# Half of the first 40 up blocks in plain f32, 16 activations kept on chip, and lists, gathers and loads re-paced

## The chip, the cores and the metric

The kernel runs on one core of one Trainium2 chip. The metric is the device time of one execution in microseconds (us); several executions are timed and their median is taken. One more execution is recorded by the hardware profiler, and every row below is from that one.

## The reference

One decoder layer over 512 tokens of width 1024. First comes attention with its output product and a layer norm; the change does not touch that part. Then comes a memory of 16384 experts, of which every token uses 16 for each of 8 heads:

```python
q = (hx @ w_pq).reshape(PEER_CHUNK, PEER_HEADS, 2, PEER_HALF)
sc = jnp.einsum('thpd,hpnd->thpn', q, sub_keys).astype(jnp.float32)
v_half, i_half = lax.top_k(sc, PEER_TOPK)
cand = v_half[:, :, 0, :, None] + v_half[:, :, 1, None, :]
...
top_s, top_pos = lax.top_k(cand, PEER_TOPK)
idx = jnp.take_along_axis(cand_idx, top_pos, axis=-1)
g = jax.nn.softmax(top_s, axis=-1)
a = jax.nn.gelu(jnp.einsum('thkd,td->thk', u_tab[idx], hx), approximate=False)
return jnp.einsum('thk,thkd->td', (g * a).astype(hx.dtype), v_tab[idx])
```

The layer ends with a second layer norm of `alpha * x + gate2 * ffn`.

## The kernel before, in words

The expert part treats the tokens in two ways. For 128 tokens ("tile 0") and for 64 tokens ("the half tile") the chosen rows of `u_tab` and `v_tab` are gathered: GpSimd (POOL) issues one indirect DMA of 128 rows (512 KB) into one of five buffers `gb`, and VectorE (DVE) makes one dot product with it (L746, for u) or one multiply-add into `acc0` (L782, for v). The half tile needs 64 dots only, tile 0 needs 128 dots and 128 multiply-adds. For the other 320 tokens (and for the v side of the half tile, so 384 there) the kernel computes all experts densely, in 128 blocks of 128 experts:

- **U loop.** For each block e the rows `u_T[e]` are loaded to `raw` (SP queue, three buffers). ScalarE (ACT) rounds them to `hi` (fp32r), DVE makes `lo = raw - hi` (three buffers each; an instruction carries the line of the helper, L86 and L87). TensorE (PE) multiplies three times for each of 8 slices of the width (hi by h2h, hi by h2l, lo by h2h; `mm3`, L96 to L98), 24 matmuls of 128x320 into a bank `st`, of which there are four. ACT takes the gelu (L812). The first NB = 32 results stay on chip as `a_r`; the other 96 (`a_s`) are written to DRAM (`a_d`).
- **Beside the U loop** generators are pulled by amounts of a budget for each block: `tk` makes the four lists of chosen experts (token tiles in the order 1, 2, 3, 0, all on DVE), `gt` issues the gathers with their dots (the half tile as soon as list 1 is there, tile 0 when list 0 is there), and `gg` builds the dense weights g of tiles 2, 3 and 1 with one-hot products (DVE `oh`, ACT `go` and `stage`, PE f32 matmuls at L692) and writes them to `g_d`.
- **V loop.** For each block n, in the order of a list `order`, `v_blk` is loaded to `raw` and split as above. The weights of a group of 8 blocks come with one DMA of 1.5 MB from `g_d` on ACT's queue (`gl`, two buffers), issued one group ahead. ACT and DVE make `w = a * gl` (the a comes from `a_r`, or from DRAM by `a_b`), then `wh` and `wl`, and PE does 18 matmuls of 128x512 into six banks that are kept over all blocks.
- **End.** For the last six blocks all splits are made first; the last four go to `hi4` and `lo4`. PE then completes one token tile after the other, and `finish` does the layer norm of each on DVE. `finish(0)`, of tile 0, is given out at n = 116, after all the remaining multiply-adds.

Each engine runs its instructions in one order, set when the program is built, and waits at each for what it reads and for free buffers.

Of the kernel before, what the change touches and what calls it, by code (L numbers as in the profile page):

```python
# [20 lines left out]
P = 128  # L21
# [12 lines left out]
ALPHA = 2.0 ** 0.25  # L34
LAM0 = 0.8 - 0.6 * math.exp(-0.0)
LOWEST = -3.0e38
NB = 32
GB = 8
NS = 96
GRATE = 0.52  # L40
HU = 64
T0U = P + HU
TU = S - T0U
LAST = 6
GBUF = 5
RA = 1.7
RB = 1.9


@with_exitstack  # L50
def layer(ctx: ExitStack, tc: tile.TileContext, A, out, dbg=None):
# [43 lines left out]
    def mm3(ps, lh, ll, rh, rl, first, last):  # L95
        nc.tensor.matmul(ps, lh, rh, start=first, stop=False)  # L96
        nc.tensor.matmul(ps, lh, rl, start=False, stop=False)  # L97
        nc.tensor.matmul(ps, ll, rh, start=False, stop=last)  # L98
# [76 lines left out]
    def drain(g, n=None):  # L175
        i = 0
        while n is None or i < n:
            try:
                next(g)
            except StopIteration:  # L180
                return False
            i += 1
        return True
# [391 lines left out]
    def u_split(e):  # L575
        return split(load_raw(A["u_T"][e], [P, KB, P]), [P, KB, P])

    prev = None
    for b in range(16):
        raw = load_raw(A["w_pqT"][b], [P, KB, P])  # L580
        hi, lo = split(raw, [P, KB, P])
        ps = bank()
        for k in range(KB):
            mm3(ps, hi[:, k, :], lo[:, k, :], h2h[:, k, :], h2l[:, k, :], k == 0, k == KB - 1)
        qT = pq.tile([P, S], F32, name="qT", tag="qT", bufs=3)
        nc.scalar.copy(qT, ps)
        if b >= 14:
            early[b - 14] = u_split(b - 14)
        if prev:
            scores(*prev)  # L590
        prev = (b, qT)
# [208 lines left out]
        return us  # L800

    def u_block(e):
        hi, lo = early.pop(e) if e in early else u_split(e)
        ps = psq[0].tile([P, TU], F32, name="st", tag="st", bufs=psq[1])
        for k in range(KB):
            mm3(ps, hi[:, k, :], lo[:, k, :], h2h[:, k, T0U:], h2l[:, k, T0U:], k == 0, k == KB - 1)
        pace[0], pace_next[0] = pace_next[0], split.last
        if NB <= e < NB + NS:
            a = ring.tile([P, TU], F32, name="a_s", tag="a_s", bufs=3)
        else:  # L810
            a = ring.tile([P, TU], F32, name="a_r", tag="a_r", bufs=NB)
        nc.scalar.activation(a, ps, AF.Gelu)  # L812
        acts[e] = a

    def keep(e):
        if NB <= e < NB + NS:
            nc.scalar.dma_start(a_d[e - NB], acts[e])
            acts[e] = None

    g_stack = ExitStack()  # L820
    gp = g_stack.enter_context(tc.tile_pool(name="gp", bufs=1, reuse_waits="tile"))
    tk = all_topk(gp)
    gg = all_g(gp, tk)
    c1 = c2 = 0.0
    gt = gathers()
    for e in range(NB + NS):
        u_block(e)
        keep(e)
        budget[0] = pull(tk, budget[0] + (2.6 if 1 not in best else 1.6))
        if 2 in best:  # L830
            c1 += GRATE
            while c1 >= 1.0:
                c1 -= 1.0
                drain(gg, 1)
        if 1 in lists:
            c2 = pull(gt, c2 + (RA if not weighted else RB))
    pull(tk, 1e9)
    while not weighted:
        next(gt)
    drain(gg)  # L840
    g_stack.close()
    sel_stack.close()
    psB_stack.close()
    psq[:] = ctx.enter_context(tc.tile_pool(name="psC", bufs=1, space=bass.MemoryType.PSUM, reuse_waits="tile")), 2, 6

# [3 lines left out]
    order = list(range(NB)) + list(range(NB + NS, NKEY)) + list(range(NB, NB + NS))  # L849

    def g_load(e):
        gl = vp.tile([P, NTG, GB * TG], F32, name="gl", tag="gl", bufs=2)
        nc.scalar.dma_start(gl, g_d.rearrange("g p i t -> p g (i t)")[:, :, e * TG:(e + GB) * TG])
        return gl

# [37 lines left out]
    for n in range(NKEY):  # L893
        if n % GB == 0 and n + GB < NKEY:
            gls[order[n + GB]] = g_load(order[n + GB])
        if n + NB + NS < NKEY:
            u_block(n + NB + NS)
            c2 = pull(gt, c2 + 3.6)
        else:
            c2 = pull(gt, c2 + 1.6)  # L900
        if n == NKEY - 16:
            ring_stack.close()
            fin = ctx.enter_context(tc.tile_pool(name="fin", bufs=1, side="right", reuse_waits="tile"))
# [114 lines left out]
```

## Time and profile before

| what | value |
|---|---|
| median of 3 runs | 1553.13 us (1549.42 to 1555.18) |
| the profiled execution, device time | 1551.68 us |
| its span, first to last instruction | 1549.9 us |
| busy in the span | PE 1432.2, DVE 1267.8, ACT 826.1, POOL 466.8 us |
| moved by DMA | 451.43 MB, mean 291 GB/s |

The span falls into stages: up to about 360 us attention, the queries and their scores; from 360 to about 981 us the U loop; from there to about 1540 us the V loop and its end. A busy time is the union of an engine's instructions, so an engine that is busy for a whole stretch may be what sets its length; "idle before" in a row is the time that the engine stood still just ahead of the instruction, with what ended it.

### The profile page before, as it was taken

How to read it: one execution, taken by the hardware profiler on the slowest of the kernel's cores; microseconds unless marked ns; L12 is line 12 of the kernel's file. 1: busy time of each engine (PE TensorE's matmuls, PEld its weight loads, DVE VectorE, ACT ScalarE, POOL GpSimd, SP SyncE). 2: the span in 40 equal slices, each digit the busy share in tenths (PEclk: the TensorE clock that was granted, in tenths of full speed). 3: DMA queues.
4: the chain of work that ended last, by engine and by line, in shares of the span. 5: the costliest groups of instructions: out<-in, count | busy, mean ns of one | idle time of the engine just before them, and what ended most of it. 6: DMA issues, size and time to landing. Idle time of an engine off the chain costs nothing.

```text
span 1549.9 us, 22874 instructions
## 1 busy us (share of the span) xinstructions
PE 1432.2 (92%) x7837; PEld 1254.3 (81%) x7837; DVE 1267.8 (82%) x2606; ACT 826.1 (53%) x1523; POOL 466.8 (30%) x338
## 2 busy tenths in 40 slices
PE   6999998998688899999999969999989999989996
PEld 5777776888687889999999969888868778868884
DVE  7897676999888998798879848989778788879766
ACT  2465534334357889899799834344333343334440
POOL 0000000000433334454544525545434443532000
PEclk9999998999999999999999989999989999999998
DMA  8856363222767789999999999999999999999751
GB/s 312 289 182 200 130 212 103 83 85 92 250 239 283 238 310 375 357 408 394 416 342 390 405 362 409 382 379 346 340 385 342 368 372 355 363 337 362 233 171 48
DMA packets 184855, 451.43 MB, mean 291 GB/s; under 512 B 15841, under 2 KB 90977, under 8 KB 181538
## 3 DMA queue, kind: packets, MB, share of 16 engines
q1 hardware_dynamic: 75426, 241.28, 43.0%
q0 software_dynamic: 46080, 167.79, 28.9%
q10 hardware_dynamic: 63232, 40.90, 8.7%
q8 instruction: 61, 1.00, 0.3%
q14 instruction: 56, 0.46, 0.1%
HBM read 404.00 MB, written 45.88 MB: 290 GB/s over the span
## 4 chain that ended last, share of the span: by engine, by line
PE 47%; issue 14%; DMA 13%; DVE 11%; POOL 8%; ACT 5%; POOLq 0%; SPq 0%; DVEq 0%; ACTq 0%
POOL gb L741 8%; PE acc L97 7%; PE acc L98 7%; PE acc L96 7%; DMA raw<-v_blk 5%; PE bank L96 5%; PE bank L97 4%; PE bank L98 4%; DMA gl<-g_d 3%; DMA raw<-u_T 3%; DVE lo L87 3%; PE st L96 2%; PE st L98 2%; PE st L97 2%; ACT hi L86 2%
## 5 line engine op out<-in xcount | busy, mean ns | idle before, releaser
L86 ACT CAST hi<-raw 128x1024 fp32r<-128x1024 f32 x286 | 299.8, 1050 | 333.5 <-DMA raw<-v_blk 111.4
L87 DVE TENSOR_TENSOR lo<-raw,hi 128x1024 fp32r<-128x1024 f32 x286 | 348.7, 1221 | 119.0 <-ACT hi L86 113.4
L96 PE MATMUL st<-h2h,hi 128*128 128x320 f32 x1024 | 326.3, 319 | 27.6 <-ACT hi L86 27.6
L98 PE MATMUL st<-h2h,lo 128*128 128x320 f32 x1024 | 322.0, 316 | 17.5 <-DVE lo L87 17.5
L97 PE MATMUL st<-h2l,hi 128*128 128x320 f32 x1024 | 321.7, 314 | 0.0
L96 PE MATMUL acc<-hi,wh 128*128 128x512 f32 x768 | 302.2, 394 | 17.3 <-ACT hi L86 17.0
L97 PE MATMUL acc<-lo,wh 128*128 128x512 f32 x768 | 303.8, 396 | 5.0 <-DVE lo L87 4.6
L98 PE MATMUL acc<-hi,wl 128*128 128x512 f32 x768 | 301.8, 393 | 0.0
L741 POOL DMA_INDIRECT gb<-v_tab,ei x128 | 182.4, 1425 | 240.2 <-DVE acc L782 222.3
L746 DVE SCALAR_TENSOR_TENSOR gb<-gb,h2n 128x1024 f32<-128x1024 f32 x192 | 230.7, 1218 | 21.2 <-DMA gb<-u_tab,ei 15.4
L741 POOL DMA_INDIRECT gb<-u_tab,ei x128 | 183.4, 1433 | 196.5 <-DVE gb L746 182.1
L96 PEld LDWEIGHTS st<-h2h,hi 128*128 128x128 f32 x1024 | 196.5, 192 | 31.2 <-ACT hi L86 31.2
L98 PEld LDWEIGHTS st<-h2h,lo 128*128 128x128 f32 x1024 | 196.0, 192 | 20.5 <-DVE lo L87 20.5
L97 PEld LDWEIGHTS st<-h2l,hi 128*128 128x128 f32 x1024 | 196.3, 192 | 0.0
L96 PEld LDWEIGHTS acc<-hi,wh 128*128 128x128 f32 x768 | 145.9, 190 | 49.8 <-ACT hi L86 18.7
L97 PEld LDWEIGHTS acc<-lo,wh 128*128 128x128 f32 x768 | 145.8, 190 | 41.7 <-DVE lo L87 10.4
L688 ACT ACTIVATE go<-oh,iT 128x128 f32<-128x128 bf16 x384 | 169.7, 525 | 9.4 <-DVE oh L682 7.5
L741 POOL DMA_INDIRECT gb<-u_tab,eip x64 | 91.0, 1422 | 272.1 <-ACT hi L86 148.7
L98 PEld LDWEIGHTS acc<-hi,wl 128*128 128x128 f32 x768 | 145.9, 190 | 30.3
L782 DVE SCALAR_TENSOR_TENSOR acc<-gb,w,acc 128x1024 f32<-128x1024 f32 x127 | 162.2, 1277 | 0.0
L104 POOL TENSOR_TENSOR rs_r<-rs_v,mhalf 128x1 f32<-128x1 f32 (+1 forms) x12 | 9.3, 775 | 364.1 <-DVE rs_v L102 328.3
L692 PE MATMUL acc<-go,oh 128*128 128x128 f32 x768 | 108.5, 284 | 7.3 <-ACT go L688 7.1
(213 smaller groups left out, 1988.9 us busy)
## 6 DMA issues: line engine op xcount, KB each, us to landing
raw<-u_T SPq DMA_DIRECT2D x128, 512.0 KB
raw<-v_blk SPq DMA_DIRECT2D x128, 512.0 KB
wada<-w_adaT SPq DMA_DIRECT2D x48, 512.0 KB
g_d<-stage SPq DMA_DIRECT2D x24, 1024.0 KB
gl<-g_d ACTq DMA_DIRECT2D x16, 1536.0 KB
a_d<-a_s ACTq DMA_DIRECT2D x96, 160.0 KB
a_b<-a_d SPq DMA_DIRECT2D x96, 160.0 KB
raw<-w_pqT SPq DMA_DIRECT2D x16, 512.0 KB
```

The lines of the kernel that those rows point to most:

```text
L86: nc.scalar.copy(hi, src)
L87: split.last = nc.vector.tensor_sub(lo, src, hi.bitcast(F32))
L96: nc.tensor.matmul(ps, lh, rh, start=first, stop=False)
L97: nc.tensor.matmul(ps, lh, rl, start=False, stop=False)
L98: nc.tensor.matmul(ps, ll, rh, start=False, stop=last)
L104: nc.gpsimd.tensor_tensor(r, v, mhalf.to_broadcast([P, n]), op=OP.pow)
L688: nc.scalar.activation(go[:, i, :], oh0[:, :, i], AF.Copy, scale=iT[:, 2, t0 + i:t0 + i + 1])
L692: nc.tensor.matmul(ps[:, i * P:(i + 1) * P], oh1[:, 4 * u + i, :], go[:, 4 * u + i, :], start=True, stop=True)
L741: nc.gpsimd.indirect_dma_start(out=b, out_offset=None, in_=A[tab], in_offset=bass.IndirectOffsetOnAxis(ap=idx[:, j:j + 1], axis=0))
L746: paced(nc.vector.scalar_tensor_tensor(b, b, 1.0, h2n, op0=OP.mult, op1=OP.mult, accum_out=acc))
L782: paced(nc.vector.scalar_tensor_tensor(acc0, b, w0[:, j:j + 1], acc0, op0=OP.mult, op1=OP.add))
```

## The change

- Of the first 40 U blocks (`PLAIN`) the odd ones are not split. PE multiplies the loaded `raw`, as f32, by `h2f`, an f32 copy of the activations: 8 f32 matmuls of 128x320 where there were 24 fp32r ones, no `hi` on ACT, no `lo` on DVE. `h2f` is made once by a DVE addition over 128x2560. The two blocks that are split early, in the stage of the queries, are now 0 and 2.
- NB goes from 32 to 24 and NS from 96 to 88. The last 16 U blocks keep their results on chip (`a_l`, in memory that the lists and g leave free at e = 112), so 88 results go through DRAM. In the V loop the order is 24 from `a_r`, 16 from `a_l`, 88 from DRAM.
- After list 2 is made the lists are pulled at 0.7 a block (before 1.6), so lists 3 and 0 come later. The build of g goes at 0.54 (before 0.52), the half tile's dots at 1.6 (1.7), tile 0's multiply-adds in the V loop at 1.45 (1.6).
- `gl` has one buffer for groups with an even number; odd groups are loaded to `gl2`, in the memory that h2h had. The numbers of the groups in their order are 0, 1, 2, 14, 15, 3, 4, and so on, so that groups 2 and 14 share one buffer, one after the other, and so do 15 and 3. `hi4` has that same memory.

```diff
@@ -34,17 +34,19 @@
 ALPHA = 2.0 ** 0.25
 LAM0 = 0.8 - 0.6 * math.exp(-0.0)
 LOWEST = -3.0e38
-NB = 32
+NB = 24
 GB = 8
-NS = 96
-GRATE = 0.52
+NS = 88
+GRATE = 0.54
 HU = 64
 T0U = P + HU
 TU = S - T0U
 LAST = 6
 GBUF = 5
-RA = 1.7
+RA = 1.6
 RB = 1.9
+RV = 1.45
+PLAIN = 40
 
 
 @with_exitstack
@@ -585,7 +587,7 @@
         qT = pq.tile([P, S], F32, name="qT", tag="qT", bufs=3)
         nc.scalar.copy(qT, ps)
         if b >= 14:
-            early[b - 14] = u_split(b - 14)
+            early[2 * b - 28] = u_split(2 * b - 28)
         if prev:
             scores(*prev)
         prev = (b, qT)
@@ -800,15 +802,22 @@
         return us
 
     def u_block(e):
-        hi, lo = early.pop(e) if e in early else u_split(e)
         ps = psq[0].tile([P, TU], F32, name="st", tag="st", bufs=psq[1])
-        for k in range(KB):
-            mm3(ps, hi[:, k, :], lo[:, k, :], h2h[:, k, T0U:], h2l[:, k, T0U:], k == 0, k == KB - 1)
-        pace[0], pace_next[0] = pace_next[0], split.last
+        if e < PLAIN and e % 2:
+            raw = load_raw(A["u_T"][e], [P, KB, P])
+            for k in range(KB):
+                nc.tensor.matmul(ps, raw[:, k, :], h2f[:, k, :], start=k == 0, stop=k == KB - 1)
+        else:
+            hi, lo = early.pop(e) if e in early else u_split(e)
+            for k in range(KB):
+                mm3(ps, hi[:, k, :], lo[:, k, :], h2h[:, k, T0U:], h2l[:, k, T0U:], k == 0, k == KB - 1)
+            pace[0], pace_next[0] = pace_next[0], split.last
         if NB <= e < NB + NS:
             a = ring.tile([P, TU], F32, name="a_s", tag="a_s", bufs=3)
+        elif e < NB:
+            a = ring.tile([P, TU], F32, name="a_r", tag="a_r", bufs=NB)
         else:
-            a = ring.tile([P, TU], F32, name="a_r", tag="a_r", bufs=NB)
+            a = late[0].tile([P, TU], F32, name="a_l", tag="a_l", bufs=NKEY - NB - NS)
         nc.scalar.activation(a, ps, AF.Gelu)
         acts[e] = a
 
@@ -816,6 +825,9 @@
         if NB <= e < NB + NS:
             nc.scalar.dma_start(a_d[e - NB], acts[e])
             acts[e] = None
+
+    h2f = ring.tile([P, KB, TU], F32, name="h2f")
+    nc.vector.tensor_add(h2f, h2h[:, :, T0U:].bitcast(F32), h2l[:, :, T0U:].bitcast(F32))
 
     g_stack = ExitStack()
     gp = g_stack.enter_context(tc.tile_pool(name="gp", bufs=1, reuse_waits="tile"))
@@ -823,23 +835,27 @@
     gg = all_g(gp, tk)
     c1 = c2 = 0.0
     gt = gathers()
-    for e in range(NB + NS):
+    late = []
+    for e in range(NKEY):
+        if e == NB + NS:
+            pull(tk, 1e9)
+            while not weighted:
+                next(gt)
+            drain(gg)
+            g_stack.close()
+            sel_stack.close()
+            late.append(ctx.enter_context(tc.tile_pool(name="late", bufs=1, reuse_waits="tile")))
         u_block(e)
         keep(e)
-        budget[0] = pull(tk, budget[0] + (2.6 if 1 not in best else 1.6))
-        if 2 in best:
+        if e < NB + NS:
+            budget[0] = pull(tk, budget[0] + (2.6 if 1 not in best else 1.6 if 2 not in best else 0.7))
+        if 2 in best and e < NB + NS:
             c1 += GRATE
             while c1 >= 1.0:
                 c1 -= 1.0
                 drain(gg, 1)
         if 1 in lists:
             c2 = pull(gt, c2 + (RA if not weighted else RB))
-    pull(tk, 1e9)
-    while not weighted:
-        next(gt)
-    drain(gg)
-    g_stack.close()
-    sel_stack.close()
     psB_stack.close()
     psq[:] = ctx.enter_context(tc.tile_pool(name="psC", bufs=1, space=bass.MemoryType.PSUM, reuse_waits="tile")), 2, 6
 
@@ -849,7 +865,10 @@
     order = list(range(NB)) + list(range(NB + NS, NKEY)) + list(range(NB, NB + NS))
 
     def g_load(e):
-        gl = vp.tile([P, NTG, GB * TG], F32, name="gl", tag="gl", bufs=2)
+        if e // GB % 2 == 0:
+            gl = vp.tile([P, NTG, GB * TG], F32, name="gl", tag="gl", bufs=1)
+        else:
+            gl = hpool.tile([P, NTG, GB * TG], F32, name="gl2", tag="hh")
         nc.scalar.dma_start(gl, g_d.rearrange("g p i t -> p g (i t)")[:, :, e * TG:(e + GB) * TG])
         return gl
 
@@ -893,11 +912,7 @@
     for n in range(NKEY):
         if n % GB == 0 and n + GB < NKEY:
             gls[order[n + GB]] = g_load(order[n + GB])
-        if n + NB + NS < NKEY:
-            u_block(n + NB + NS)
-            c2 = pull(gt, c2 + 3.6)
-        else:
-            c2 = pull(gt, c2 + 1.6)
+        c2 = pull(gt, c2 + RV)
         if n == NKEY - 16:
             ring_stack.close()
             fin = ctx.enter_context(tc.tile_pool(name="fin", bufs=1, side="right", reuse_waits="tile"))
```

Three places of the program's order, before and after. The first is PE's order at the start of the U loop (`st` is a block's bank, hi and lo its split). Before, block 0 is followed by block 1:

```order
L97 MATMUL st_3518<-h2l_2089,hi_3378 128x320
L98 MATMUL st_3518<-h2h_2088,lo_3379 128x320
L96 MATMUL st_3563<-h2h_2088,hi_3444 128x320
L97 MATMUL st_3563<-h2l_2089,hi_3444 128x320
L98 MATMUL st_3563<-h2h_2088,lo_3445 128x320
```

Now:

```order
L99 MATMUL st_3512<-h2l_2081,hi_3370 128x320
L100 MATMUL st_3512<-h2h_2080,lo_3371 128x320
L809 MATMUL st_3557<-h2f_3507,raw_3558 128x320 x8
L98 MATMUL st_3590<-h2h_2080,hi_3436 128x320
L99 MATMUL st_3590<-h2l_2081,hi_3436 128x320
```

What was 24 matmuls of block 1 is one row of 8, which read `h2f` and the load itself, between two split blocks.

The second is ACT's order where the load of the group for n = 24 to 31 is issued (`w` takes its first 64 columns from `gl` by a COPY, hi is the split of a v block). Before, this comes at n = 15:

```order
L86 CAST hi_10458<-raw_10456 128x1024
L874 COPY w_10567<-gl_10027 128x64
L853 DMA gl_10592<-g_d_179 128x24x128
L86 CAST hi_10495<-raw_10493 128x1024
L86 CAST hi_10529<-raw_10527 128x1024
L880 CAST wh_10536<-w_10533 128x384
L880 CAST wh_10570<-w_10567 128x384
L86 CAST hi_10563<-raw_10561 128x1024
L874 COPY w_10606<-gl_10310 128x64
L874 COPY w_10640<-gl_10310 128x64
```

Now it comes at n = 23:

```order
L899 CAST wh_10306<-w_10303 128x384
L88 CAST hi_10265<-raw_10263 128x1024
L893 COPY w_10371<-gl_9842 128x64
L872 DMA gl_10119<-g_d_171 128x24x128
L88 CAST hi_10299<-raw_10297 128x1024
L88 CAST hi_10333<-raw_10331 128x1024
L899 CAST wh_10340<-w_10337 128x384
L899 CAST wh_10374<-w_10371 128x384
L893 COPY w_10407<-gl_10119 128x64
L88 CAST hi_10367<-raw_10365 128x1024
```

Before, the DMA (gl_10592) stands eight blocks ahead of its use, and the COPY for block 16 (from gl_10310) reads an older load. Now the COPY for block 24 reads gl_10119, whose DMA stands five rows above it, behind the last COPY from gl_9842, which has the same buffer; the hi of block 23 stands behind that COPY.

The third is DVE's order where tile 0's last multiply-adds and the start of `finish(0)` stand (h2n is its output buffer, w and wl belong to the v blocks). Before, lo_13848 is that of n = 112:

```order
L782 SCALAR_TENSOR_TENSOR acc0_3512<-gb_13878,w0_3514,acc0_3512 128x1024
L87 TENSOR_TENSOR lo_13810<-raw_13807,hi_13809 128x1024
L875 TENSOR_TENSOR w_13889<-a_b_13887,gl_13541 128x320
L782 SCALAR_TENSOR_TENSOR acc0_3512<-gb_13914,w0_3514,acc0_3512 128x1024
L881 TENSOR_TENSOR wl_13893<-w_13889,wh_13892 128x384
L875 TENSOR_TENSOR w_13925<-a_b_13923,gl_13541 128x320
L87 TENSOR_TENSOR lo_13848<-raw_13845,hi_13847 128x1024
L875 TENSOR_TENSOR w_13958<-a_b_13956,gl_13541 128x320
L921 TENSOR_TENSOR h2n_3513<-acc0_3512,g2r_14121 128x512 x2
L922 SCALAR_TENSOR_TENSOR h2n_3513<-xr0_14127,h2n_3513 128x512
L881 TENSOR_TENSOR wl_13929<-w_13925,wh_13928 128x384
L87 TENSOR_TENSOR lo_13884<-raw_13881,hi_13883 128x1024
```

Now, lo_14033 is that of n = 121 and lo_14066 that of n = 122:

```order
L894 TENSOR_TENSOR w_14005<-a_b_14003,gl2_13610 128x320
L784 SCALAR_TENSOR_TENSOR acc0_3504<-gb_13830,w0_3506,acc0_3504 128x1024
L900 TENSOR_TENSOR wl_14009<-w_14005,wh_14008 128x384
L784 SCALAR_TENSOR_TENSOR acc0_3504<-gb_13833,w0_3506,acc0_3504 128x1024
L89 TENSOR_TENSOR lo_14033<-raw_14030,hi_14032 128x1024
L784 SCALAR_TENSOR_TENSOR acc0_3504<-gb_13836,w0_3506,acc0_3504 128x1024
L894 TENSOR_TENSOR w_14038<-a_b_14036,gl2_13610 128x320
L784 SCALAR_TENSOR_TENSOR acc0_3504<-gb_13839,w0_3506,acc0_3504 128x1024
L900 TENSOR_TENSOR wl_14042<-w_14038,wh_14041 128x384
L784 SCALAR_TENSOR_TENSOR acc0_3504<-gb_13842,w0_3506,acc0_3504 128x1024
L89 TENSOR_TENSOR lo_14066<-raw_14063,hi_14065 128x1024
L936 TENSOR_TENSOR h2n_3505<-acc0_3504,g2r_13622 128x512 x2
```

Before, the last multiply-add stands ahead of the lo of block 112. Now they stand two or three to a block up to the lo of block 122, and `finish(0)` comes behind that.

## Rows read from the trace of the kernel before

**Rows 1.** The page's head.
```profile
span 1549.9 us, 22874 instructions
```
**Rows 2.** Windows: start:end, length, busy us (instructions) by engine, clock, DMA share, GB/s.
```profile
360.00:580.00 220.00, 184.13 (x1153) 173.35 (x1153) 202.63 (x605) 141.52 (x217) 75.80 (x53) 0.95 0.70 242
580.00:900.00 320.00, 317.60 (x2284) 315.02 (x2284) 271.55 (x359) 284.19 (x512) 157.39 (x108) 1.00 1.00 387
...
980.00:1120.00 140.00, 138.76 (x610) 113.98 (x609) 122.72 (x158) 55.72 (x101) 67.05 (x47) 1.00 1.00 363
1120.00:1400.00 280.00, 259.45 (x1096) 209.54 (x1095) 224.21 (x266) 103.33 (x184) 116.21 (x83) 0.96 1.01 358
1400.00:1500.00 100.00, 100.00 (x442) 82.80 (x442) 73.70 (x102) 42.73 (x78) 8.16 (x6) 1.00 0.78 259
```
**Rows 3.** Groups of DVE instructions, 360 to 580 us: count, busy us, mean ns, idle before.
```profile
L746 DVE SCALAR_TENSOR_TENSOR gb<-gb,h2n 128x1024 f32<-128x1024 f32 x48 | 57.9, 1213 | 4.1 <-DMA gb<-u_tab,eip 4.1
L87 DVE TENSOR_TENSOR lo<-raw,hi 128x1024 fp32r<-128x1024 f32 x38 | 46.2, 1216 | 0.3 <-ACT hi L86 0.3
L684 DVE TENSOR_TENSOR oh<-iT,iota 128x1024 f32<-128x1024 f32 x13 | 15.8, 1215 | 0.0
...
L682 DVE TENSOR_TENSOR oh<-iTb,iota 128x1024 bf16<-128x1024 bf16 x13 | 8.8, 680 | 0.0
```
**Rows 4.** Timeline of PE in a U block: start, duration.
```profile
620.11 0.31 PE L97 MATMUL st<-h2l,hi 128*128 128x320 f32 x1
...
622.31 0.31 PE L97 MATMUL st<-h2l,hi 128*128 128x320 f32 x1
```
**Rows 5.** Timeline of PE at eight f32 records of 128x128.
```profile
268.46 1.06 PE L567 MATMUL bank<-skT,qT 128*128 128x128 f32 x8
269.27 0.48 PE L96 MATMUL bank<-h2h,hi 128*128 128x512 f32 x1
```
**Rows 6.** Groups of PE instructions by shape: f32 matmuls of other widths.
```profile
L270 PE MATMUL bank<-qk 64*128 64x512 f32 x16 | 4.5, 641 | 0.1
...
L270 PE MATMUL bank<-qk 64*128 64x128 f32 x16 | 2.3, 316 | 0.0
```
**Rows 7.** The gelu's line: duration ns min/median/max, first and last start.
```profile
L812 ACT ACTIVATE a_s<-st x96: 410/432/483, 541.3 to 980.8; 128x320 f32<-128x320 f32 x96
...
L812 ACT ACTIVATE a_r<-st x32: 410/438/464, 365.9 to 533.2; 128x320 f32<-128x320 f32 x32
```
**Rows 8.** Timeline of SP: a load of a u block is issued.
```profile
474.94 0.81 SPq L92 DMA_DIRECT2D raw<-u_T  x1
```
**Rows 9.** Timeline of ACT: the split of that block.
```profile
481.43 1.06 ACT L86 CAST hi<-raw 128x1024 fp32r<-128x1024 f32 x1 [3.07 <-DMA raw<-u_T]
```
**Rows 10.** Timeline of ACT: the first g load is issued.
```profile
913.09 0.39 ACTq L853 DMA_DIRECT2D gl<-g_d  x1
```
**Rows 11.** Timeline of DVE: the first use of that load.
```profile
925.29 0.49 DVE L875 TENSOR_TENSOR w<-a_r,gl 128x320 f32<-128x320 f32 x1 [17.63 <-DMA gl<-g_d]
```
**Rows 12.** Timeline of ACT at a later g load.
```profile
1095.04 0.40 ACTq L853 DMA_DIRECT2D gl<-g_d  x1
...
1129.67 1.04 ACT L86 CAST hi<-raw 128x1024 fp32r<-128x1024 f32 x1 [9.21 <-DMA raw<-v_blk]
```
**Rows 13.** Waits of SP's queue in the V loop: total us, times, longest.
```profile
SPq L871 <- DMA gl<-g_d: 54.9, 6, 14.5
...
SPq L911 <- DMA gl<-g_d: 20.0, 1, 20.0
```
**Rows 14.** Groups of DVE instructions, 1400 to 1549 us.
```profile
L881 DVE TENSOR_TENSOR wl<-w,wh 128x384 fp32r<-128x384 f32 x31 | 17.1, 553 | 24.2 <-ACT wh L880 24.2
L875 DVE TENSOR_TENSOR w<-a_b,gl 128x320 f32<-128x320 f32 x30 | 14.6, 487 | 0.5
L782 DVE SCALAR_TENSOR_TENSOR acc<-gb,w,acc 128x1024 f32<-128x1024 f32 x10 | 12.8, 1276 | 0.0
...
L928 DVE TENSOR_TENSOR h2n<-h2n,ln2g 128x512 f32<-128x512 f32 x2 | 1.4, 687 | 0.0
```

## Prediction

> **What bounds the kernel now.** I read the windows first, since one average over the span hides that the stages have different limits. From 360 to 580 us, the first 40 U blocks, DVE is busy 202.63 of 220 us and PE only 184.13; DMA moves 242 GB/s at a share of 0.70 [rows 2]. So there the vector engine sets the pace, and the gelu's line gives it: 32 gelus start between 365.9 and 533.2 us, 5.40 us a block [rows 7]. From 580 to 900 us PE is busy 317.60 of 320 us, and DVE has 48 us to spare: PE sets the pace (and DMA, at a share of 1.00 and 387 GB/s, is not far off) [rows 2]. In the V loop PE is busy 138.76 of 140, then 259.45 of 280, then 100.00 of 100 us [rows 2]: PE sets the pace, but the middle window loses 20.5 us to idle time, and some 11 more to a clock of 0.96 (4% of 280; after an idle stretch the granted clock is at its lower level for a while). The view of SP's waits says what the idle time is about: loads of a_b stood 54.9 us in six waits for a g load, one other 20.0 us [rows 13].
>
> **The U loop, first 40 blocks.** What DVE does there: 57.9 us dots, 46.2 lo's, 15.8 + 8.8 one-hots [rows 3]. The rest of its 202.63 is 73.9 us, of which some 4 read out the dots; 70 are the four lists, 17.5 each. The change takes 20 lo's away (20 x 1.216 = 24.3 us), and at 0.7 a block list 0 moves behind block 40 (17.5). DVE is left with about 161 us. It is no longer the bound.
>
> PE is. A split block is 24 matmuls; 15 of them take 622.31 - 620.11 = 2.20 us [rows 4], 0.147 each, 3.52 a block. A plain block is 8 f32 matmuls, for which no row of this shape exists. Eight f32 records of 128 columns start in 0.81 us [rows 5], 0.101 each, and every f32 matmul leaves two records. The mean time of an f32 record grows by (641 - 316) / 384 = 0.846 ns a column [rows 6], so a record of 320 takes 0.101 + 192 x 0.000846 = 0.263 us, and a block 16 x 0.263 = 4.21: PE gets 0.69 us longer a block. From below, 16 records at an fp32r matmul's 0.147 give 2.35 us; from above, with no overlap at all between records, the whole mean of 316 + 192 x 0.846 = 478 ns gives 7.65. I take 4.21, because both rows from which it comes are f32 matmuls, and rows 5 shows them overlapping. PE then has 184.13 + 20 x 0.69 = 198 us of work.
>
> The Trainium skill ("FP8 and Floating Point Precision", section "TensorE Precision Notes") says that true FP32 takes four passes through the array, where the split takes three; if a pass costs the same in both, a plain block takes 4/3 of 3.52, an estimate of 4.69 us, and the sum 10 us more. Rows 5 and 6 agree in kind (two records to a matmul, about two clocks to a column in each) and give a little less.
>
> A new wait comes with it: a plain block holds its `raw` until PE has ended it, where a split one frees it at its lo. With three buffers the load of block e waits for PE's end of block e - 3. A load issued at 474.94 [rows 8] ends ACT's wait at 481.43 [rows 9], 6.5 us later; with hi (1.05) and lo (1.22) behind it that is 8.8 us. PE has blocks e - 2 and e - 1 meanwhile, 3.52 + 4.21 = 7.7, and g's matmuls. It shows as 0 to 1 us at every second block, not more. What is queued behind a late hi on ACT is the gelu of the block before, and PE has four banks. So the stretch takes a little more than PE's work: I take 203 us of 220, **-17 us** (-26 if the pace falls to that of blocks 40 on, 4.63 by the gelus of rows 7, for most of the blocks; -6 if the loads are late at each).
>
> `h2f` is one addition over 2560 columns, 2.5 x 1.22 = 3.05 us on DVE, in the stage of the queries; the scores and first lists behind it on DVE wait as long. PE and the w_pq splits hide part: **+1** (0 to +3).
>
> **The rest of U.** Blocks 40 to 110 are PE's; list 0 now lies there, but tile 0's dots begin some 12 blocks later, and DVE's 48 us of room take the difference: 0. At e = 112 the memory of g is freed, so all of g must be written before the last 16 gelus: g's build ends near e = 107 as before, and the wait for its last DMA was there before too. 16 writes less to DRAM are off PE's path: **-2** (-5 to +5).
>
> **The V loop.** A block is 18 matmuls; 442 take 100.00 us [rows 2], 0.226 each, 4.07 a block, which stays. What changes is where it waits.
>
> *The g loads.* With one buffer for two neighbours, the load of the group at n = 24 can be issued only when w of block 23 is made (second place of the order), and the same at n = 40; hi4 waits likewise for w of the last block. The row between is the hi of block 23: it stands behind the COPY that waits for the load. Between the load's issue and the time at which PE lacks block 23 there are four blocks, 16 us. A load takes at least 12.2 us (issued 913.09, used 925.29) [rows 10, 11] and at most 34.6 (issued 1095.04; the hi of a v load queued behind it comes at 1129.67) [rows 12]. Traffic is lighter now at n = 24, as the first 40 blocks fetch no a_b. I take 21, so 5 us of idle PE and about as much by the clock, 10 in all at n = 24 (0 to 18), and 4 at n = 40. The group at n = 8 can come only when h2h is free, at the end of U; it has six blocks, 24 us, for it: 1 (0 to 11). What goes is the loss at the load of rows 12, when the last layer norm's inputs were fetched beside it: I put 13 of the 33 us on it (ACT's 9.21 and some 4 by the clock). Those inputs now come at n = 24 itself and are in the 10.
>
> *Traffic.* With RV = 1.45 a block has 1.45 / 1.2 = 1.21 gathers of 512 KB, before 1.33. At DMA shares of 1.00 and 363, 358 GB/s [rows 2] that shortens the later stalls; of the roughly 20 us that are left of the middle window's loss I take 13.
>
> *The end.* Tile 0's multiply-adds now start near n = 27 and 19 or 20 are left at n = 116; the third place of the order shows them between the lo's of blocks 112 to 122. DVE's own work for a block is 1.22 + 0.487 + 0.553 = 2.26 us, a multiply-add 1.276 [rows 14]. With 17 in blocks 112 to 119 that is 4.97 us a block against PE's 4.07, 7 us too much; three each in 120 and 121 make 6.1, 4 more; `finish(0)` (five pairs at 1.4 [rows 14] and one pass more, 8 us) then stands ahead of the last splits. Of these 19 us the lead of three blocks that DVE has over PE covers some 10: **+9** (3 to 20). It is the term I trust least. Before, all of this lay in blocks with room: the window from 1400 shows DVE at 73.70 of 100 us [rows 2].
>
> Sum of V: 10 + 4 + 1 + 13 + 9 = 37 against 33 of before (1.2 + 20.5 + 11), which I round down to **+2**, since the lighter traffic helps the short waits too (-10 to +30).
>
> All together -17 + 1 - 2 + 2 = **-16 us**. The profiled execution took 1551.68 us (its span is 1549.9 [rows 1]), so 1535.7; it lies 1.4 us under the median of the runs, so the median should be 1537.
>
> **Rivals.** What can be told from no change here is 0.5%, 7.8 us.
>
> (a) *Each f32 record costs two whole fp32r matmuls.* Then a plain block is 8 x 4 x 0.147 = 4.70 us, PE has 24 us more in the first 40 blocks instead of 14, and the time is 1547 if nothing covers it, 1542 if half is covered. For: two records to a matmul. Against: rows 5 and 6, by which a record is 0.263 and not 0.294. Chance 0.12. This is what the rule on four passes in the Trainium skill's "FP8 and Floating Point Precision" would come to.
>
> (b) *The end gives the gain back.* Multiply-adds and `finish(0)` delay the last lo's by their full 19 us, and 1.9 gathers a block in n = 112 to 122 meet a DMA that is already at 259 GB/s without them [rows 2]: +10 on my sum, 1547. Chance 0.22, no measurable change.
>
> (c) *The g loads in one buffer decide, and it gets slower.* If each of the three takes the 34.6 us of rows 12, PE lacks 11 + 18 + 18 = 47 us where I have 15: 1569. It is slower by over 0.5% from 39 us on, that is from loads of 31 us on. For: SP's waits for such loads were up to 20.0 us with the load issued eight blocks ahead [rows 13]. Against: 12.2 us in rows 10 and 11, and less traffic. Chance 0.13; 0.04 more for a plain block of over 5.8 us, at which PE's 184 + 20 x 2.3 would exceed the 220 us of now by 10.
>
> (d) *More gain.* The U pace goes to -26, and the lighter traffic takes the later V stalls away (-13): 1518. For: PE reached 317.60 of 320 with all its loads at a DMA share of 1.00. Chance 0.12.
>
> My forecast holds the remaining 0.37, with its own range of 1529 to 1545. Faster is that, (d) and most of (a): 0.60; within 0.5% is (b) and the rest of (a): 0.23; slower 0.17. For 8 in 10 the range leaves out the far ends of (c) and (d): 1518 to 1562.
>
> **What would show it.** Right: in the first 40 blocks about 5.05 us from gelu to gelu, DVE with 160 of 203 us busy and PE near full; plain records 0.26 us apart; ACT waiting for a g load near n = 23 and PE idle about 5 us there; DVE without idle time from n = 112 on. Wrong: a plain record at 0.29 us or more, hi's of U blocks that wait over 2 us for `raw` each, PE idle for 20 us at n = 24 or n = 40, or an end in which the time from the last v block to the last instruction grows by over 20 us.

## The result

The changed kernel takes 1565.64 us (median of 20 runs, 1556.36 to 1574.69), the kernel before on the same chips 1555.18 us (1549.19 to 1561.81): a ratio of 1.0069, 95% interval 1.0052 to 1.0086. It is slower, by some 11 us, where I had forecast 16 us less. The profiled execution took 1565.12 us (span 1563.3).

The same windows as in [rows 2], now of the changed kernel:

```profile
360.00:580.00 220.00, 194.52 (x1033) 165.79 (x1032) 185.97 (x610) 126.18 (x213) 68.13 (x53) 0.94 0.72 253
580.00:900.00 320.00, 317.43 (x2253) 312.14 (x2252) 248.55 (x324) 277.76 (x495) 126.17 (x86) 1.00 0.92 352
980.00:1120.00 140.00, 131.53 (x568) 107.02 (x568) 105.76 (x157) 51.77 (x93) 52.41 (x38) 0.98 0.97 343
1120.00:1400.00 280.00, 274.86 (x1194) 225.90 (x1193) 235.05 (x285) 112.38 (x201) 129.99 (x82) 0.99 1.00 358
1400.00:1500.00 100.00, 92.99 (x392) 73.77 (x391) 77.47 (x90) 34.80 (x60) 45.87 (x31) 0.98 0.96 338
```

DVE went from 202.63 to 185.97 us busy in the first window, so it is no longer the bound there, and PE from 184.13 to 194.52; yet the window holds about the same 40 blocks. In the V loop the middle window is better (PE 274.86 against 259.45), those from 980 and 1400 on are worse (131.53 against 138.76, 92.99 against 100.00). The gelu's line, against [rows 7]:

```profile
L821 ACT ACTIVATE a_s<-st x88: 410/431/509, 496.5 to 924.8; 128x320 f32<-128x320 f32 x88
...
L821 ACT ACTIVATE a_r<-st x24: 417/432/475, 370.8 to 490.1; 128x320 f32<-128x320 f32 x24
L821 ACT ACTIVATE a_l<-st x16: 422/430/438, 928.3 to 984.0; 128x320 f32<-128x320 f32 x16
```

From single gelus and the first matmul of single V blocks in the two timelines the spans divide so (us):

| stretch | before | changed | forecast of the difference | measured |
|---|---|---|---|---|
| first 40 U blocks | 217.7 | 214.8 | -17 | -3 |
| U block 40 to the first V block | 394.8 | 394.5 | -2 | 0 |
| V blocks 0 to 112 | 491.1 | 481.4 | -7 | -10 |
| V block 112 to the end | 80.5 | 101.8 | +9 | +21 |

(My +1 for h2f lies ahead of the first gelu, where the changed profile has 5 us more; that is not told from scatter: the first gelu starts between 363.4 and 371.3 us in all the profiles of this study.)

**Where the U loop's gain went.** Among the waits in 360 to 580 us (total, times, longest), ACT's for the load of a U block, before

```profile
ACT hi L86 <- DMA raw<-u_T: 14.7, 8, 3.2
```

and now

```profile
ACT hi L88 <- DMA raw<-u_T: 65.8, 12, 10.1
DVE lo L89 <- ACT hi L88: 19.1, 11, 4.2
...
PE acc L694 <- ACT go L690: 10.9, 2, 8.7
...
PE acc L694 <- DVE cand L557: 6.2, 1, 6.2
```

SP, which issues the loads, stood 26.9 us for the ends of plain blocks:

```profile
SPq L94 <- PE st L809: 26.9, 6, 10.8
```

So plain blocks hold loads, ACT's hi is late by it, and so is DVE's lo, which had waited 0.3 us for hi before [rows 3]. A piece of the timelines shows one such load. PE, at a plain block (L809) and at what follows it in its order, a product for g:

```profile
510.01 4.47 PE L809 MATMUL st<-h2f,raw 128*128 128x320 f32 x16
523.15 1.22 PE L694 MATMUL acc<-go,oh 128*128 128x128 f32 x4 [8.66 <-ACT go L690]
```

SP, at the next load:

```profile
514.51 0.33 SPq L94 DMA_DIRECT2D raw<-u_T  x1
```

ACT, from there to the `go` that the product reads:

```profile
512.94 1.06 ACT L697 COPY stage<-acc 128x512 f32<-128x512 f32 x1 [0.99 <-ACT a_s L821]
518.03 1.04 ACT L88 CAST hi<-raw 128x1024 fp32r<-128x1024 f32 x1 [4.03 <-DMA raw<-u_T]
518.98 1.03 ACT L697 COPY stage<-acc 128x512 f32<-128x512 f32 x1
520.03 1.28 ACT L658 ACT_TABLE_LOAD   x1
521.32 0.31 ACT L658 ACTIVATE g<-g 128x128 f32<-128x128 f32 x1
522.58 1.35 ACT L690 ACTIVATE go<-oh,iT 128x128 f32<-128x128 bf16 x3 [0.94 <-DVE eq L650]
```

The plain block ends at about 514.5. Only then is its buffer free, and the load is issued at 514.51. ACT stands 4.03 us for it, splits it at 518.03, and then does what stands behind the split in its order: a copy of `stage`, the softmax of list 0 with its table load, and at 522.58 the `go`. PE, whose next instruction in its order is the product that reads this go, stands 8.66 us.

Not all of that is the load's. At 522.58 go had waited 0.94 us more for DVE (`eq`, a step of list 3), and DVE had worked since 502.08 without a pause of 0.1 us. All eight searches of list 0 stand ahead of that `eq` in DVE's order, the last at 517.59. In e6 below, where the plain blocks have buffers of their own, two of them do, and the same product waits 4.36 us:

```profile
513.07 1.22 PE L694 MATMUL acc<-go,oh 128*128 128x128 f32 x4 [4.36 <-ACT go L690]
```

So here the late load and the lists' place in DVE's order are mixed, and this piece doesn't tell them apart. At g's first product the load's part can be read by itself. The one-hot that go reads is made on DVE at 458.32, but go stands behind a late hi and starts 2.5 us after the one-hot is there:

```profile
458.32 0.69 DVE L684 TENSOR_TENSOR oh<-iTb,iota 128x1024 bf16<-128x1024 bf16 x1
```
```profile
460.57 1.04 ACT L88 CAST hi<-raw 128x1024 fp32r<-128x1024 f32 x1 [5.43 <-DMA raw<-u_T]
461.52 3.42 ACT L690 ACTIVATE go<-oh,iT 128x128 f32<-128x128 bf16 x8
```
```profile
462.09 2.29 PE L694 MATMUL acc<-go,oh 128*128 128x128 f32 x9 [6.24 <-DVE cand L557]
```

A late load thus holds PE through what stands behind the split on ACT as well, not through the split alone.

**Where V's loss is.** The load for n = 24 and what it holds, on ACT:

```profile
1060.22 0.38 ACTq L872 DMA_DIRECT2D gl<-g_d  x1
...
1065.68 0.92 ACT L899 CAST wh<-w 128x384 fp32r<-128x384 f32 x2
1082.00 0.24 ACT L893 COPY w<-gl 128x64 f32<-128x64 f32 x1 [15.39 <-DMA gl<-g_d]
1082.15 1.04 ACT L88 CAST hi<-raw 128x1024 fp32r<-128x1024 f32 x1
```

Issued at 1060.22, and its first reader starts at 1082.00: 21.8 us, and the hi of block 23 directly behind it. That is the 21 us that I had taken from [rows 10 to 12]. PE, behind it:

```profile
1083.24 0.79 PE L98 MATMUL acc<-hi,wh 128*128 128x512 f32 x1 [6.31 <-ACT hi L88]
```

Near the end, all engines from 1490 to 1527 us, and DVE's rows:

```profile
1490.00:1527.00 37.00, 29.67 (x114) 20.80 (x114) 35.73 (x50) 11.68 (x23) 9.72 (x9) 0.95 0.72 269
```
```profile
1480.67 1.23 DVE L89 TENSOR_TENSOR lo<-raw,hi 128x1024 fp32r<-128x1024 f32 x1 [7.11 <-ACT hi L88]
...
1506.66 1.29 DVE L784 SCALAR_TENSOR_TENSOR acc<-gb,w,acc 128x1024 f32<-128x1024 f32 x1
1507.85 0.50 DVE L894 TENSOR_TENSOR w<-a_b,gl 128x320 f32<-128x320 f32 x1
1508.25 1.29 DVE L784 SCALAR_TENSOR_TENSOR acc<-gb,w,acc 128x1024 f32<-128x1024 f32 x1
1509.45 0.57 DVE L900 TENSOR_TENSOR wl<-w,wh 128x384 fp32r<-128x384 f32 x1
1509.91 1.30 DVE L784 SCALAR_TENSOR_TENSOR acc<-gb,w,acc 128x1024 f32<-128x1024 f32 x1
1511.11 1.24 DVE L89 TENSOR_TENSOR lo<-raw,hi 128x1024 fp32r<-128x1024 f32 x1
1512.24 1.31 DVE L936 TENSOR_TENSOR h2n<-acc,g2r 128x512 f32<-128x512 f32 x2
1513.45 1.31 DVE L937 SCALAR_TENSOR_TENSOR h2n<-xr,h2n 128x512 f32<-128x512 f32 x2
1514.65 1.30 DVE L113 BATCH_NORM_STATS2 ln_st<-h2n 128x6 f32<-128x512 f32 x2
```

DVE is busy 35.73 of 37 us, PE 29.67: DVE has just stood 7.11 us for a split, and then has two or three late multiply-adds to each block, and finish(0) (h2n) ahead of the last splits. Before, DVE was busy 73.70 of the 100 us from 1400 [rows 2]. Among the waits from 1466 to 1530 us the chain is seen: PE waits for wh, and wh for DVE's w.

```profile
ACT wh L899 <- DVE w L894: 16.5, 8, 6.1
...
PE acc L98 <- ACT wh L899: 6.3, 5, 3.2
```

From 1490 to 1527 us neither PE nor DVE nor ACT waits for a load, so there it is DVE's work that holds PE and not the gathers' traffic.

### The profile page after: what moved, and what is told of

Same layout as the page of the kernel before. It is cut to its first block, busy times and chain, and to the rows that moved or that the text cites. A ratio compares the mean times of both kernels' runs of the same rounds, so it can differ in the third digit from the quotient of the medians.

```text
span 1563.3 us, 22401 instructions
## 1 busy us (share of the span) xinstructions
PE 1446.1 (93%) x7677; PEld 1245.4 (80%) x7677; DVE 1246.2 (80%) x2587; ACT 804.2 (51%) x1503; POOL 476.0 (30%) x338
## 4 chain that ended last, share of the span: by engine, by line
PE 30%; issue 21%; POOL 14%; DMA 13%; DVE 13%; ACT 8%; SPq 0%; POOLq 0%; DVEq 0%; ACTq 0%
POOL gb L743 14%; DMA gl<-g_d 4%; PE bank L98 4%; ACT go L690 4%; PE bank L100 4%; PE bank L99 4%; DVE lo L89 3%; PE st L98 2%; PE st L99 2%; PE st L100 2%; DMA raw<-u_T 2%; PE acc L694 2%; PE acc L99 2%; PE acc L98 2%; PE acc L100 2%
## 5 line engine op out<-in xcount | busy, mean ns | idle before, releaser
L88 ACT CAST hi<-raw 128x1024 fp32r<-128x1024 f32 x266 | 278.5, 1050 | 353.6 <-DMA raw<-v_blk 116.3
L89 DVE TENSOR_TENSOR lo<-raw,hi 128x1024 fp32r<-128x1024 f32 x266 | 325.1, 1224 | 159.3 <-ACT hi L88 158.6
L98 PE MATMUL st<-h2h,hi 128*128 128x320 f32 x864 | 277.3, 321 | 9.4 <-ACT hi L88 9.4
L100 PE MATMUL st<-h2h,lo 128*128 128x320 f32 x864 | 271.2, 314 | 11.2 <-DVE lo L89 11.2
L743 POOL DMA_INDIRECT gb<-v_tab,ei x128 | 199.7, 1560 | 247.0 <-DVE acc L784 213.1
L99 PE MATMUL st<-h2l,hi 128*128 128x320 f32 x864 | 270.5, 313 | 0.0
L100 PEld LDWEIGHTS st<-h2h,lo 128*128 128x128 f32 x864 | 164.7, 191 | 12.9 <-DVE lo L89 12.9
L98 PEld LDWEIGHTS st<-h2h,hi 128*128 128x128 f32 x864 | 165.2, 191 | 10.9 <-ACT hi L88 9.8
L99 PEld LDWEIGHTS st<-h2l,hi 128*128 128x128 f32 x864 | 165.0, 191 | 1.1
L694 PE MATMUL acc<-go,oh 128*128 128x128 f32 x768 | 107.7, 287 | 19.1 <-ACT go L690 12.6
L694 PEld LDWEIGHTS acc<-go,oh 128*128 128x128 f32 x768 | 98.3, 196 | 26.3 <-ACT go L690 22.7
```

What stands on the lines that cost most here:

```text
L88: nc.scalar.copy(hi, src)
L89: split.last = nc.vector.tensor_sub(lo, src, hi.bitcast(F32))
L694: nc.tensor.matmul(ps[:, i * P:(i + 1) * P], oh1[:, 4 * u + i, :], go[:, 4 * u + i, :], start=True, stop=True)
L743: nc.gpsimd.indirect_dma_start(out=b, out_offset=None, in_=A[tab], in_offset=bass.IndirectOffsetOnAxis(ap=idx[:, j:j + 1], axis=0))
```

## The experiments

Ratios are to the kernel before on the same chip, with the 95% interval; each row's stretches come from its own profile (us).

| kernel | ratio | first 40 U | to first V | V 0 to 112 | 112 to end |
|---|---|---|---|---|---|
| before | 1 | 217.7 | 394.8 | 491.1 | 80.5 |
| changed | 1.0069 (1.0052 to 1.0086) | 214.8 | 394.5 | 481.4 | 101.8 |
| e1_noplain | 1.0028 (1.0008 to 1.0048) | 194.7 | 397.4 | 483.5 | 96.3 |
| e2_lists16 | 0.9973 (0.9951 to 0.9995) | 207.7 | 395.3 | 492.2 | 80.6 |
| e3_galt | 1.0023 (0.9998 to 1.0047) | 212.9 | 393.3 | 484.6 | 96.3 |
| e4_rb24 | 1.0177 (1.0145 to 1.0209) | 214.3 | 427.5 | 490.1 | 80.3 |
| e5_nb16 | 0.9996 (0.9972 to 1.0021) | 213.6 | 395.4 | 483.7 | 94.9 |
| e6_nb16_rawp | 0.9944 (0.9919 to 0.9969) | 199.2 | 396.3 | 480.8 | 97.1 |
| e7_nb16_rawp_lists16 | 0.9835 (0.9801 to 0.9869) | 199.2 | 389.4 | 486.2 | 80.6 |
| e8_noplain_lists16 | 1.0031 (1.0004 to 1.0058) | 214.0 | 402.5 | 488.3 | 83.5 |
| e9_finish_late | 1.0048 (1.0023 to 1.0073) | 215.7 | 393.1 | 490.1 | 95.8 |
| e10_nb16_split_lists16 | 0.9999 (0.9977 to 1.0020) | 213.9 | 402.1 | 481.5 | 80.6 |
| e11_nb16_plain_lists16 | 0.9897 (0.9865 to 0.9930) | 209.0 | 398.7 | 482.8 | 80.4 |
| e12_noplain_again | one execution | 194.7 | 400.2 | 493.3 | 97.8 |
| e13_after_again | one execution | 213.4 | 395.2 | 489.9 | 98.1 |

In the two kernels that were profiled twice the first stretch repeats to 0.1 and 1.4 us, the second to 0.7 and 2.8, the last to 1.5 and 3.7; V's blocks 0 to 112 differ by 8.5 and 9.8.

**e1_noplain: every block split, the rest as changed.**

```diff
-PLAIN = 40
+PLAIN = 0
```

(the early splits are blocks 0 and 1, and h2f is not made)

> The changed kernel with all 128 U blocks split again (no plain f32 block, no h2f; early splits are blocks 0 and 1 again); everything else as changed. Theory A (a plain block holds its raw buffer until PE ends it, the next load is late, ACT's hi waits and go behind it, and PE waits for go): ACT's wait for raw of 65.8 us in 360 to 580 falls to some 15 us, but DVE has 24 us more to do, so the stretch takes what it took with the plain blocks, 211 to 219 us; total 1560 to 1568. Theory B (the plain blocks do give their 17 us and the later lists take them back): the stretch gets 15 us longer, total 1578 to 1585.

Neither: without plain blocks the stretch is 194.7 us, 20 less than with them. The kernel as a whole is 0.4% faster than the changed one by the two ratios. Its profile was of its fastest execution, 12 us under its median, so I took a second one.

**e12_noplain_again and e13_after_again: the same two once more.** No edit.

> The kernel of the first experiment (all blocks split, late lists) once more, for a second profile: its first one was of its fastest execution, 12 us under its median. If late lists alone speed the first 40 blocks up as that profile shows, they take 192 to 198 us again. If that was a lucky execution, 203 to 215 us, and the shared loads of the plain blocks cost less than the 20 us between the two first profiles.

> The changed kernel itself once more, for a second profile. The loads that PE holds are part of the program, so the first 40 blocks take 212 to 218 us again, and the time from V block 112 to the end 95 to 102 us. If either differs by over 5 us, the first profile was not typical and its stages can't be read to that accuracy.

194.7 again, and 213.4. The stretch is what the programs make it; the second profile of the all-split kernel is 9.6 us longer than its first, and V has about that much more (493.3 instead of 483.5). So with every block split the stretch is 23 us shorter than before, 19 of them by the later lists (e8 below, the same with lists at 1.6, has 214.0), and the plain blocks as they were made took 20 of these back.

**e2_lists16: lists at 1.6 throughout.**

```diff
-budget[0] = pull(tk, budget[0] + (2.6 if 1 not in best else 1.6 if 2 not in best else 0.7))
+budget[0] = pull(tk, budget[0] + (2.6 if 1 not in best else 1.6))
```

> The changed kernel with the lists pulled at 1.6 a block throughout, as before the change. Theory A (late loads): PE's waits in the first 40 blocks stay, DVE has 17 us more in them and is still not the bound; stretch within 5 us of 215, total 1563 to 1571. Theory B (the lists that now run beside g's build take the gain): the waits of PE for go and for DVE cand go, stretch 200 to 205, total 1550 to 1556.

The total, 1547.78 us, is B's side and lower still, but not for B's reason: the profile gains 7 us in the first 40 blocks (207.7, not B's 200 to 205), and 21 at the end of V (80.6, where the kernel before has 80.5). List 0 is complete sooner (the last step of its numbers on DVE starts at 544 us, in the changed kernel at 675), so tile 0's dots and multiply-adds are too, and 5 multiply-adds are left behind block 112 where the changed kernel has 22.

**e3_galt: the two late groups swapped, so that even and odd alternate.**

```diff
-order = list(range(NB)) + list(range(NB + NS, NKEY)) + list(range(NB, NB + NS))
+order = (list(range(NB)) + list(range(NKEY - GB, NKEY)) + list(range(NB + NS, NKEY - GB))
+         + list(range(NB, NB + NS)))
```

> The changed kernel with the two groups of the late activations swapped in V's order (groups 0, 1, 2, 15, 14, 3, ...), so that even and odd groups alternate and no g load has to wait for the group just before it. Theory A (one buffer for two neighbours costs the 9 us at n = 23 and the 3 us at n = 40): 10 to 13 us less, total 1552 to 1557. Rival (the stall is the fetch of the last layer norm's inputs and comes anyway): 0 to 4 us less, total 1561 to 1566.

0.46% less than the changed kernel by the ratios, 7 us: between the two (the median, 1556.36, lies in A's range, but the kernel before was 1.6 us faster on this chip as well). The stall at n = 23 is gone from the profile, but PE stands at the load for n = 8, which the first profile of the changed kernel did not show (its second has 3.69 us there):

```profile
1000.33 0.49 PE L98 MATMUL acc<-hi,wh 128*128 128x512 f32 x1 [4.21 <-ACT hi L88]
```

**e4_rb24: tile 0's dots faster in the U loop.**

```diff
-RB = 1.9
+RB = 2.4
```

> The changed kernel with tile 0's dots pulled at 2.4 a block in the U loop (1.9 in the change), so that its multiply-adds start some 20 blocks sooner and end before n = 116. Theory A (the end of V lost 16 us in blocks 116 to 123 and 5 behind them to the multiply-adds and finish(0) on DVE): 15 to 21 us less, total 1545 to 1551. Rival (the gathers only move, and make loads late elsewhere): 0 to 7 us less, total 1559 to 1566.

Both wrong in the sum, A right in the place: the end takes 80.3 us, 21 less, but the U loop behind block 40 takes 427.5, 33 more. Its window against the second of the result's:

```profile
580.00:900.00 320.00, 305.34 (x2130) 298.21 (x2130) 255.04 (x340) 268.92 (x481) 135.71 (x96) 0.98 0.93 353
```

PE lost 12 us there and more behind it. The dots were moved to where PE was the bound, and what they delay there costs more than the end did. Which of their claims (DVE or the loads beside the gathers) does it, no run tells apart.

**e5 to e7: 16 activations kept from the start, then two buffers for the plain blocks, then the lists at 1.6.** The control e5 frees the memory:

```diff
-NB = 24
+NB = 16
...
-NS = 88
+NS = 96
```

e6 adds, in the plain branch of `u_block`,

```diff
-            raw = load_raw(A["u_T"][e], [P, KB, P])
+            raw = ring.tile([P, KB, P], F32, name="rawp", tag="rawp", bufs=2)
+            dma(raw, A["u_T"][e])
```

and e7 adds e2's edit.

> A control for the next two: the changed kernel with 16 activations kept from the start and 96 through DRAM (24 and 88 in the change). This frees 10 KB a partition and makes the order of the groups 0, 1, 14, 15, 2, 3, ..., where even and odd alternate. Both theories: the stalls at n = 23 and n = 40 go as in the run with the swapped groups, the first 40 U blocks stay at 213 to 217 us; 1553 to 1560 where before runs at 1554.

> The control with two raw buffers of their own for the plain blocks, so that the load of a split block waits only for a lo, as before the change. Theory A (the load that is held until PE ends a plain block makes hi late, go stands behind hi on ACT, PE waits for go): ACT's 60 us of waits for raw in the first 40 blocks fall under 20, PE's waits for go vanish, the stretch takes 195 to 203 us, 12 to 20 less than the control's. Theory B (the lists, now late, are what g's build and PE wait for): the stretch stays within 5 us of the control's.

> The same with the lists at 1.6 a block throughout, so that list 0 is ready and tile 0's dots start as early as before the change. If loads and late lists are the two causes, and independent: the stretch at 195 to 205 us and the end of V without its 16 + 5 us, 1530 to 1540. Rival (with DVE's 17 us of lists back, DVE is the bound of the stretch again): 210 to 216 us, 1545 to 1550.

The control did as expected, but for a stall of 4.58 us at block 18 in place of the one at 23. With buffers of their own the plain blocks' stretch is 199.2 us instead of 213.6, as theory A had it, and ACT's wait is nearly gone (B, as a rival to A, is out):

```profile
ACT hi L88 <- DMA raw<-u_T: 4.0, 1, 4.0
```

PE's waits for go did not vanish (6.7 us in two; 10.9 in the changed kernel). Two things besides the holding differ between the two runs. With two buffers added there are five in all where there were three, and a pool of five for both kinds of block was not run. And the order on DVE is built otherwise: two of list 0's searches ahead of the first `eq` of list 3 in e6, eight in e5 and the changed kernel.

e7 is the fastest kernel here, 1527.07 us, 1.65% under the kernel before and 3 us under its range. Its windows from 360 and 1400 us:

```profile
360.00:580.00 220.00, 208.34 (x1156) 178.78 (x1155) 199.76 (x609) 147.03 (x247) 78.28 (x58) 0.98 0.80 283
...
1400.00:1500.00 100.00, 99.61 (x437) 81.53 (x436) 88.78 (x120) 39.58 (x70) 22.73 (x17) 1.00 0.75 264
```

PE is busy 208.34 of 220 and 99.61 of 100 us. DVE, with 199.76 of 220 in the first, did not bind again.

**e8_noplain_lists16: split blocks, lists at 1.6.** e1's and e2's edits together.

> The changed kernel without plain blocks and with the lists at 1.6 throughout: of the change only the late activations, the g loads in one buffer and the slower rates of the gathers are left. The stretch is DVE's again, 213 to 220 us; the end of V is clean; the stalls at n = 23 and 40 stay: 1552 to 1562 where before runs at 1554. If instead the stretch is under 205 us, DVE was not what bound it before.

214.0 us and a total as expected: DVE, busy 198 us of the 214, binds again.

**e9_finish_late: finish(0) behind the last v block.**

```diff
-            finish(0, (acc0[:, 0:512], acc0[:, 512:1024]))
         blk = v_block(n)
...
             last.append(blk)
+    finish(0, (acc0[:, 0:512], acc0[:, 512:1024]))
```

> The changed kernel with finish(0) given out behind the last v block instead of ahead of it at n = 116; the late multiply-adds stay. If the 21 us lost at the end are DVE's queue, the 8 us of finish(0) ahead of the splits of blocks 123 to 127 are part of them: blocks 112 to 127 take 71 to 75 us instead of 79, the rest behind them at most 23, total 4 to 8 less than the change (1556 to 1560 where before runs at 1554). If the gathers' traffic or the shared memory of hi4 delays the end, nothing changes: 1562 to 1566.

The ratio is 0.2% under the changed kernel's, the two intervals overlap, and the end takes 95.8 us against 101.8 and 98.1: at most a part, and not clear of the scatter. The larger part is the multiply-adds: where at most 5 of them are left for it (e2, e4, e7) the end takes 80 to 81 us. hi4 and its memory are the same in those, so the wait for that memory is no cause.

**e10 and e11: e7 with every block split; e7 with the shared buffers.** e10 is e5's edit with e1's and e2's, e11 is e5's with e2's.

> The best kernel so far (16 kept activations, two raw buffers for plain blocks, lists at 1.6; 1527) with every block split again, no h2f: its difference to that kernel is what plain blocks with buffers of their own are worth. Theory (the plain blocks are worth their price only when their loads are not held): stretch of the first 40 blocks 212 to 218 us against 199, total 12 to 25 us more, 1540 to 1553. Rival (the gain came from the lists and the groups' order): 1525 to 1533.

> The best kernel with the plain blocks in the three shared raw buffers, as in the change. Theory (the shared buffers take the plain blocks' gain): stretch 206 to 213 us, ACT's waits for raw over 40 us, total 8 to 15 us more than 1527, 1535 to 1542. Rival: within 4 us of 1527.

Both as expected: against e7 the shared buffers cost 0.6% (10 us by the ratios), and split blocks 1.6% (25 us, of which 15 are in the first 40 blocks; in the profiles 13 more lie between U block 40 and the first V block, 402.1 against 389.4 us, and no run explains them). All six cases of the first 40 blocks together (us):

| | lists late (0.7) | lists at 1.6 |
|---|---|---|
| all blocks split | 194.7 | 214 (before: 217.7) |
| plain, shared raw buffers | 213 to 216 | 208, 209 |
| plain, buffers of their own | 199.2 | 199.2 |

"Late" is not the same work in each row. With every block split nearly all of list 0 moves behind block 40 (in e1 its searches run from 560 to 599 us, and block 40's gelu starts at 564). With plain blocks its searches stay in the stretch, and only what follows them moves: the list is complete at 675 us in the changed kernel, at 567 before.

## Why the prediction was wrong

Two terms hold nearly all of the distance between the forecast and the result: 14 us in the first 40 blocks and 12 at the end of V.

**The place of the bound: right.** DVE set the pace of the first 40 blocks, and less work for it shortens them: 194.7 us with late lists and split blocks (DVE is then busy 183.71 us of the 195 from 370 on, PE 176.47), 199.2 with plain blocks that have buffers.

**A plain block's price: right.** Sixteen records of L809 take 4.47 us from the first start to the last end (the row at 510.01); with a duration of 0.43 for the last that is (4.47 - 0.43) / 15 = 0.269 us a record and 4.31 a block, where I had 4.21 and, as rival (a), 4.70. The rule in the Trainium skill's "FP8 and Floating Point Precision" (section "TensorE Precision Notes") led to an estimate of 4.69; the measured block is 8% under it. At the granted clock of 1.00 (2.4 GHz) 0.269 us for 320 columns is two clocks a column, so two records fit four passes, but a pass then took 0.134 us where an fp32r matmul takes 0.147.

**The held load: the step that failed.** "It shows as 0 to 1 us at every second block, not more." I had named the wait and priced one load against two blocks of PE (8.8 against 7.7 us), with nothing but a gelu queued behind the late hi. In the run ACT stood 65.8 us for loads in twelve waits, 5.5 us each, and DVE 19.1 us for late hi's. Go stands behind hi in ACT's one order, and g's products stand in PE's order ahead of the next block, as at 462 above. The stretch gained 3 us where I had put 17. With the lists at 1.6 the shared buffers cost 10 us in it (209.0 against 199.2), with the late lists 14 (213.6 against 199.2), nearly the whole gain. Why they cost more with late lists is not shown; the searches of list 0 that the build puts ahead of `eq`, eight against two, are part of that difference and no wait for a load.

**Two cures for one bound.** I added the relief by lo's and by lists (24.3 + 17.5 us), and put the stretch at some 201 us, which is about what plain blocks with free buffers take. But they take 199.2 us with the lists at 1.6 as well: late lists won nothing there, and had still to be paid at the end. Nor did list 0 move behind block 40 as a whole, as I had it: DVE was busy 185.97 us where I had 161, with all 32 `tp` searches (FIND_INDEX8, L559) of the four lists before 580:

```profile
L559 DVE FIND_INDEX8 tp<-tv,cand 128x8 uint32<-128x80 f32 x32 | 7.4, 235 | 0.0
```

**The end of V: a term of the right kind, mis-sized.** I had 19 us of DVE's work less 10 of lead, +9; measured +21 (+18 in the second profile). The lead was not there. Before, DVE's wl was ready 11 us ahead of PE from block 112 to 121. In the changed kernel it was 3 to 8 us ahead up to block 116 and level with PE from 117 on. At 1480 DVE had stood 7 us for a hi that waited for its load, and then ran 38 us without a pause; but in the second profile, which has no such wait at that place, the lead is gone by block 117 as well. What used it up is not shown step by step; two multiply-adds a block are part of it, which make a DVE block 4.4 us at 113 and 114 against PE's 4.07. I had called it "the term I trust least", and rival (b), with its 10 us more, came near its size (+19).

**The g loads: right at n = 24.** 21.8 us for the load (I took 21), 6.31 us of idle PE there (5). The load for n = 8, which I had put at 1 us, cost nothing in the first profile and 3.69 us in the second. The middle window gained more than forecast (15.4 us of PE's idle time against 7), but V's blocks 0 to 112 as a whole (-10 against -7) differ from forecast by less than they differ between two executions.

**The rivals.** The time lies where (c) had put it, for another reason: its loads of over 31 us did not occur (the longest that the trace times took 27.9). (b) was the nearest in place. In (d) the terms come to 1537 - 9 - 13 = 1515, not 1518; no chance hangs on it.

## What to carry to other kernels

When an operand is used straight from its load, the load's buffer is held until the consumer ends; count the buffers again, and follow what stands in the same engine order behind the instruction that the late load delays, not only the instruction. Two changes that relieve the same bound need not add up (199.2 us here with the second and without it): price each against the next bound alone, and drop the one that has a cost elsewhere. When the work beside a loop is paced anew, look in the trace for where the built order has put it: here the searches of the list that was put off stayed in the stretch. Work that is put off goes to the end, and lead that earlier stalls have used up does not cover it: look at the last stretch by itself.

## What the hardware showed that I had not expected

An f32 matmul of 128x320 leaves two records, 0.269 us apart, 0.54 us for the matmul, 3.7 times an fp32r matmul's 0.147 us; for a split in two that needs three of these, f32 costs PE 22% more (4.31 against 3.52 us a block) and saves the other engines 2.3 us. The first 40 U blocks repeated to 0.1 us and 1.4 us in two executions of the same program, while its V blocks 0 to 112 differed by 8 to 10 us: most of the scatter of this kernel's time lies in the V loop, where the DMA share is 0.96 to 1.00 (0.72 in the first 40 blocks). That the share is the reason is not shown.
